# The second block's modulation as row sums on VectorE instead of matmuls on TensorE

## The chip, the cores and the metric

One core of a Trainium2 chip runs the whole program in one launch. The time is device time in microseconds (us) from the start to the end of one execution; the kernel before was timed in three runs, and a profile was taken of one further execution. The engines are TensorE (PE; its weight loads are listed as PEld), VectorE (DVE), ScalarE (ACT), GpSimd (POOL) and SyncE (SP), which here only issues DMA transfers, all of them on one queue.

## The reference

The input x is 256 tokens of 1024 features. A first block of two layers mixes them in four ways (stick-breaking attention, RWKV-7, block attention, HGRN-2), gates and sums the four branches, projects the sum out, and adds a feed-forward net with 2816 hidden columns. A second block follows, of one layer: it has latent attention and a two-directional mLSTM, and then 16 experts. All is float32.

The second block is modulated. A vector c of 1024 numbers (and c_ctx, for a context of 256 further tokens) gives six vectors of 1024 features each, the scales, shifts and gates of the second block's norms:

```
mod     = silu(c)     @ w_mod + b_mod      # w_mod: 1024 x 6144
mod_ctx = silu(c_ctx) @ w_mod + b_mod      # only scale and shift of the first norm are used
```

They depend on neither x nor the first block, so they can be computed at any time before they are used. w_mod has 25 MB, and each of its numbers is used once or twice.

## The kernel before

Activations lie with features on the partitions: x is [128, 8, 256], eight feature tiles of 256 tokens. A product takes a piece of a weight, 1024 rows by 256 columns, in two halves of 512 KB. `half_weights` (line 205) loads a half on SP's queue into one of four raw buffers, ScalarE copies it to a rounded high part (line 179 in `copy`), and VectorE, for every third half GpSimd, subtracts to get the low part (line 182 in `sub`). TensorE then does three matmuls for each pair of tiles, high by high, high by low and low by high (lines 227 to 229 in `mm3`). Raw, high and low parts have four buffers each, so at most two pieces are ready ahead of TensorE.

`layer` (line 878) runs twice. It makes the norm and the projections of the four mixers, weaves the mixers' chains with further projections (`weave`, line 867), then does the output projection (four pieces), the norm of the feed-forward net, its 22 gate and up pieces and the down projection (four column quarters of three pieces each). Layer 1 norms the context (`norm_mod` on cx) between the gate and up products and the down projection; this is where the modulation is used first. `second` (line 1180) and `moe` (line 1816) are the second block; the experts' weights, 192 pieces of 1 MB, come last.

The order of an engine's list is not quite the order of the code. The framework plans the lists at build time: it takes the instructions in the order of the code, but where an engine has nothing to do by its own estimate, it takes a later instruction whose inputs are there and whose buffers are free. On the chip each engine then runs its list strictly in order, and SP's queue of transfers is such a list.

The modulation is a generator (`modulation`, line 1130). silu(c) and silu(c_ctx) stand in two columns of zeros in `cp`, so that a matmul with 32 columns of `cp` as its weights and 256 columns of w_mod as its data (line 1155) puts a chunk's sums on two rows of one PSUM tile, in four groups of the array's columns. Each of 24 chunks takes four loads of 256 KB into buffers borrowed from other tiles (tags qk, am, t2, r2) and eight matmuls, which the profile lists as 16 records. Two rounds of 12 chunks each end in a copy, a turn by two small matmuls and an addition of b_mod. The code asks for seven chunks beside layer 0's mixers (`M0`), four ahead of layer 0's gate and up products (`M1`), the last chunk and the end of the first round at layer 1's norm, and the whole second round ahead of layer 1's gate and up products.

Of the kernel before, what the change touches and what calls it, by code (L numbers as in the profile page):

```python
# [9 lines left out]
F32 = mybir.dt.float32  # L10
# [23 lines left out]
def _const_table():  # L34
    """Masks, rotations and index tables that depend on the shapes alone."""
# [8 lines left out]
    # partial rotary, two heads of 64 on the partitions  # L44
# [16 lines left out]
    # chunks of 64 tokens on the partitions (two of them), 64 columns  # L61
# [17 lines left out]
    # partial sums of four column groups of the array: rows r, r + 32, r + 64, r + 96  # L79
# [9 lines left out]
def _const2_table():  # L89
# [3 lines left out]
    # axial rotary, two heads of 64 on the partitions  # L93
# [14 lines left out]
    # partial sums of four column groups of the array: rows r, r + 32, r + 64, r + 96  # L108
    # gate g of head h in direction d (row 8 d + 4 g + h of the sums) goes to partition 32 d + h
# [22 lines left out]
for _name, _n in [  # L132
    ("norm1_g", 16), ("norm2_g", 16), ("final_g", 8), ("mu", 16), ("w0", 4), ("a0", 4), ("k_k", 4),
    ("k_a", 4), ("r_k", 4), ("gn_w", 4), ("gn_b", 4), ("v0", 2), ("lb", 4), ("hgn", 4),
    ("c", 8), ("c_ctx", 8), ("b_mod", 48), ("norm1_2", 8), ("norm2_2", 8), ("final_2", 8),
    ("q_norm", 3), ("kv_norm", 2), ("conv_w", 40), ("conv_b", 8), ("ml_norm", 8), ("ml_skip", 8),
]:
    _PRM[_name] = (_NPRM, _n)
    _NPRM += _n


class Block:
# [53 lines left out]
    def split(self, hi, lo, src, scale=None, eng=None):  # L196
        """src = hi + lo exactly, in two parts that one pass of the array carries."""
# [7 lines left out]
    def half_weights(self, ap, parts=1):  # L205
        """A piece [128, n <= 1024] of a weight, split."""
# [12 lines left out]
    def weights(self, ap, n):  # L219
        """A piece [128, n] of a weight, split, in two halves."""  # L220
        h = n // 2
        parts = [self.half_weights(ap[:, i * h:(i + 1) * h]) for i in range(2)]
        return lambda c, w: parts[c // h](c % h, w)
# [7 lines left out]
    def proj_fm(self, ps, w, x, nk, nm, m0=0, width=None, k0=0, first=True, last=True):  # L231
        """ps[:, m*256:+256] (+)= columns m of w (feature-major), x = (hi, lo) [128, nk, 256]."""
# [7 lines left out]
    def proj_tok(self, ps, w, x, nk):  # L240
        """ps[:, j*256:+256] = tokens of tile j, 256 columns of w (token-major)."""
# [6 lines left out]
    def rstd(self, out, ps, n, eps):  # L248
        """out = (ps / n + eps) ** -0.5"""
# [3 lines left out]
    def rstd_small(self, out, ss, n, eps):  # L253
        """out = (ss / n + eps) ** -0.5, on VectorE"""
# [4 lines left out]
    def rsqrt(self, out, x):  # L259
        """out = x ** -0.5: a first guess from the exponent, then two steps of Newton's kind."""  # L260
# [11 lines left out]
    def square_sums(self, x, w=None, cols=1):  # L272
        """[128 tokens, j, c]: sums over the features of w(k)[:, c] * x ** 2, by column groups of the array."""
# [14 lines left out]
    def spread(self, r, out):  # L288
        """Factors by token [128, nj] on every partition: out [128, nj * 128] in PSUM."""
# [4 lines left out]
    def rms8(self, x):  # L294
        """(mean of x ** 2 over the 8 feature tiles + 1e-6) ** -0.5 on every partition."""
# [5 lines left out]
    def rms(self, squares, n, eps, nj=2):  # L301
        """(sum of the squares over the features / n + eps) ** -0.5 of nj * 128 tokens, on every partition."""
# [32 lines left out]
    def norm_split(self, x, nk, n, eps, gcol, hi, lo, bias=None, r=None):  # L335
        """hi + lo = x * rstd * g (+ bias), over the nk feature tiles of x."""
# [12 lines left out]
    def att_out(self, att, v, hp, hh, yhi, ylo):  # L349
        """o^T = v^T att^T of two heads; att [128 s, 2, 384]: (s0: t 0..255), (s1: t 128..255)."""  # L350
# [7 lines left out]
    def stick(self, got, y):  # L358
        """q is scaled by 1/8."""
# [29 lines left out]
    def tri(self, t):  # L389
        """Zero where s >= t in the diagonal blocks of t [128 s, 2, (t0, t1 of s0, t1 of s1)]."""  # L390
# [4 lines left out]
    def rotate(self, x, rot, cos, sin, n):  # L395
        """x [128, n, 256] in place."""
# [47 lines left out]
    def lower_bounds(self):  # L444
        """lb[:, 0:2] of layer 0, [:, 2:4] of layer 1; and 1 - lb."""
# [20 lines left out]
    def hgrn(self, l, q, f, got, room, y):  # L466
        """q, f, sg = silu(g) * 2 feature-major [128, 2, 256]; v token-major."""
# [18 lines left out]
        # scores by keys: [64 cc + s, head parity, 2 * head pair + tile, query of the same 64 tokens]; the first  # L486
        # half of a tile against its second half; the first tile against the second
# [44 lines left out]
        # sums of the products with the first 64 keys of a tile in one bank, with the others in the next  # L532
        o, v = self.mx(), got["v"]
        for hp in range(2):
            for j in range(2):
# [7 lines left out]
                # the first into each half of the partitions clears what the bank has seen before  # L543
# [21 lines left out]
    def rwkv(self, l, pz, y):  # L565
        """pz: four pieces [128, 2, 256] of the projected columns."""
# [53 lines left out]
        # unit key, key, bonus  # L620
# [25 lines left out]
        # decays within chunks of 64  # L646
# [33 lines left out]
        # instance (h, c): h = 2 hp + hh, c = 2 j + cc; its tokens lie on partitions 64 cc..  # L680
# [36 lines left out]
        def prod(lh, rh):  # L717
            """lh^T rh of each instance: both on the tokens' partitions; bank = chunk parity."""
# [7 lines left out]
        for m in (2, 4, 8, 16, 32):  # L726
            # what the chain below needs only later fills its gaps
# [34 lines left out]
        # U0 = X (A_ak V), W = X a  # L762
# [23 lines left out]
        # the state's matrices: on the features' partitions, column (cc, hp, j)  # L786
# [15 lines left out]
        # diag(P_C): eye * pc, column order (cc, hp, j)  # L802
# [64 lines left out]
    def weave(self, streams):  # L867
        """Emits the streams side by side; each comes with about its number of steps, and its start among the others."""
# [9 lines left out]
    def layer(self, l, x):  # L878
# [4 lines left out]
        if l == 0:  # L883
            # x * g for the first two products; their results take the tokens' factors
# [3 lines left out]
            for i in range(2):  # L888
                # the first weights' halves follow the halves of x that they meet
# [7 lines left out]
            # the array is cold: its sums take squares that are added before  # L897
# [11 lines left out]
        if l:  # L909
            self.mod_tags = ("qk",)  # L910
            for _ in islice(self.mods, 2):
                pass
# [90 lines left out]
        def branch(n, first):  # L1003
            """mg (+)= 2 sigmoid(gate) * (y @ w_branch) of mixer n."""
# [21 lines left out]
        if l == 0:  # L1026
            mods = self.mods = self.modulation()
            self.mod_tags = ("qk",)
            streams.append((islice(mods, M0), MO, MS))
# [5 lines left out]
        for k in range(8):  # L1035
            self.split(mh[:, k], ml[:, k], mg_[:, k], scale=0.5)
        for c in range(4):
            ps = self.acc()
# [4 lines left out]
        # the products take x * g; their results the tokens' factors  # L1043
# [4 lines left out]
        self.mod_tags = ("am", "t2", "r2", "r2")  # L1048
        for _ in islice(self.mods, M1 if l == 0 else 26):
            pass  # L1050
# [10 lines left out]
        for c in range(4):  # L1061
            ps = self.mx()
            for g, (k0, n) in enumerate(((0, 8), (8, 8), (16, 6))):
                w = self.weights(a["w_down"][l, c][:, 256 * k0:256 * (k0 + n)], 256 * n)
# [6 lines left out]

    def silu_mul(self, ps, r, hi, lo):
        """hi + lo = silu(r * ps[:, :256]) * (r * ps[:, 256:])"""
# [46 lines left out]
    def slabv(self, *dims, dt=F32, pool=None):  # L1120
        """A view of 8 KB a partition, of the slabs that stay or of the second block's."""
# [8 lines left out]
    def modulation(self):  # L1130
        """mod[:, i, 0] of c and [:, i, 1] of c_ctx: column tile i of silu(c) @ w_mod + b_mod."""
        T, S, V = self.T, self.S, self.V
        # c and c_ctx stand in columns 22 and 23 of zeros: chunk q of a round takes 32 columns so that
        # its sums go to the rows 2 q and 2 q + 1, beside those of the round's other chunks
# [935 lines left out]
```

## Time and profile before

| | |
|---|---|
| median of three runs | 1905.74 us (1903.93 to 1913.77) |
| span of the profiled execution, first to last instruction | 1908.3 us |
| TensorE's weight loads, busy | 1345.3 us (71%) |
| VectorE, busy | 916.8 us (48%) |
| ScalarE, busy | 720.2 us (38%) |
| GpSimd, busy | 456.5 us (24%) |
| mean granted TensorE clock, of full speed | 0.929 |
| bytes moved by the DMA engines | 416.91 MB, mean 218 GB/s |

The page gives nothing of the profiled execution outside its span, so the span stands for its own time; it lies between the timed runs. Busy time is the union of an engine's instructions. Matmuls overlap in the records (one of 0.28 us starts every 0.12 us), so sums of single durations are larger than busy times. Layer 0 lasts from the start to about 550 us, layer 1 from there to about 1090 us, the second block's attention and mLSTM to about 1450 us, and the experts to the end.

### The profile page before, as it was taken

What the parts mean: (1) busy time and instruction counts of PE and PEld (TensorE: products, weight loads), DVE (VectorE), ACT (ScalarE), POOL (GpSimd) and SP (SyncE); (2) the same over time, 40 slices, a digit from 0 to 9 for tenths busy, and PEclk for the clock granted to TensorE, in tenths of its full rate; (3) what the DMA queues carried; (4) which work ended last, traced back from release to release, by engine and by line L of the source; (5) the groups of instructions that cost most, each with busy time, mean ns of one, the idle gap of its engine ahead of it and who ended that gap; (6) DMA issues with size and microseconds to landing.
All of it is one profiled execution on the core that took longest, in us unless ns stands there. A gap on an engine that the chain in (4) does not pass through costs nothing. (4 is left out here: it accounts for less than half of the span.)

```text
span 1908.3 us, 34087 instructions
## 1 busy us (share of the span) xinstructions
PE 1695.0 (89%) x14380; PEld 1345.3 (71%) x14380; DVE 916.8 (48%) x1395; ACT 720.2 (38%) x1136; POOL 456.5 (24%) x285
## 2 busy tenths in 40 slices
PE   7799899999999899999999999989997976667666
PEld 7668799999989788997998998867896410101113
DVE  8755645577557756553776448453574100000001
ACT  5535544444446454543444343554443200000001
POOL 4352143244323622431442221111231000000000
PEclk9899999999999899999999999989999977776788
DMA  6552546455645226566554643322457999999997
GB/s 228 167 171 92 167 154 200 146 176 177 180 153 162 84 86 194 165 219 228 169 177 137 184 136 126 100 72 74 164 209 298 427 426 427 427 427 428 426 427 329
DMA packets 96379, 416.91 MB, mean 218 GB/s; under 512 B 10689, under 2 KB 12385, under 8 KB 71521
## 3 DMA queue, kind: packets, MB, share of 16 engines
q1 hardware_dynamic: 96224, 414.72, 60.3%
q8 instruction: 113, 1.85, 0.4%
q14 instruction: 42, 0.34, 0.1%
HBM read 413.63 MB, written 1.05 MB: 217 GB/s over the span
## 5 line engine op out<-in xcount | busy, mean ns | idle before, releaser
L227 PE MATMUL acc<-s,wh 128*128 128x256 f32 (+1 forms) x2236 | 652.3, 292 | 12.6 <-ACT wh L179 8.6
L228 PE MATMUL acc<-s,wh 128*128 128x256 f32 (+1 forms) x2236 | 647.7, 290 | 4.8 <-DVE s L191 4.0
L229 PE MATMUL acc<-s,wl 128*128 128x256 f32 (+1 forms) x2236 | 647.7, 290 | 0.0
L179 ACT ACTIVATE wh<-wr 128x1024 fp32r<-128x1024 f32 (+2 forms) x349 | 359.4, 1036 | 343.1 <-PE acc L228 203.0
L227 PEld LDWEIGHTS acc<-s,wh 128*128 128x128 f32 x2236 | 436.2, 195 | 29.1 <-issue 15.7
L228 PEld LDWEIGHTS acc<-s,wh 128*128 128x128 f32 x2236 | 436.4, 195 | 15.6 <-issue 8.0
L182 POOL TENSOR_TENSOR wl<-wr,wh 128x1024 fp32r<-128x1024 f32 (+1 forms) x115 | 282.7, 2458 | 658.5 <-ACT wh L179 589.9
L229 PEld LDWEIGHTS acc<-s,wl 128*128 128x128 f32 x2236 | 436.2, 195 | 3.8 <-issue 1.8
L182 DVE TENSOR_TENSOR wl<-wr,wh 128x1024 fp32r<-128x1024 f32 (+2 forms) x234 | 304.4, 1302 | 240.1 <-ACT wh L179 238.9
L1831 PE MATMUL mx<-s,s 128*32 128x512 f32 x608 | 103.3, 766 | 39.4 <-DMA s<-in_w_moe_dram 39.4
L1831 PE MATMUL mx<-mw,s 128*32 128x512 f32 x416 | 76.2, 809 | 36.3 <-DMA mw<-in_w_moe_dram 36.3
L1831 PEld LDWEIGHTS mx<-s,s 128*32 128x32 f32 x608 | 14.5, 120 | 112.3 <-DMA s<-in_w_moe_dram 96.3
L1831 PEld LDWEIGHTS mx<-mw,s 128*32 128x32 f32 x416 | 9.7, 122 | 92.1 <-DMA mw<-in_w_moe_dram 88.1
L188 POOL TENSOR_TENSOR t<-t,rr 128x256 f32<-128x256 f32 x44 | 42.8, 972 | 127.5 <-DVE t L188 124.8
L191 DVE SCALAR_TENSOR_TENSOR x<-acc,mod,x 128x256 f32<-128x256 f32 x28 | 12.2, 480 | 104.2 <-PE acc L1839 100.8
L188 DVE TENSOR_TENSOR m<-m,mx 128x1024 f32<-128x1024 f32 x4 | 4.9, 1222 | 114.5 <-PE mx L1831 114.5
L227 PE MATMUL mx<-r,wh 128*128 128x256 f32 x208 | 59.0, 284 | 0.0
L228 PE MATMUL mx<-r,wh 128*128 128x256 f32 x208 | 58.8, 282 | 0.0
L229 PE MATMUL mx<-r,wl 128*128 128x256 f32 x208 | 58.6, 282 | 0.0
L191 DVE SCALAR_TENSOR_TENSOR m<-m,mx 128x1024 f32<-128x1024 f32 x4 | 4.9, 1220 | 107.5 <-ACT m L1862 107.5
L1831 PE MATMUL mx<-s,ht 128*32 128x512 f32 x224 | 39.2, 794 | 17.9 <-DMA s<-in_w_moe_dram 17.8
L191 DVE SCALAR_TENSOR_TENSOR t<-t,t 128x256 f32<-128x256 f32 (+1 forms) x46 | 46.9, 1019 | 12.4 <-ACT t L1076 8.2
(516 smaller groups left out, 2534.6 us busy)
## 6 DMA issues: line engine op xcount, KB each, us to landing
s<-in_w_moe_dram SPq DMA_DIRECT2D x110, 1024.0 KB, 19.6
mw<-in_w_moe_dram SPq DMA_DIRECT2D x81, 1024.0 KB, 19.6
wr<-in_w_in_dram SPq DMA_DIRECT2D x158, 512.0 KB, 4.1
wr<-in_w_gu_dram SPq DMA_DIRECT2D x88, 512.0 KB, 4.3
wr<-in_w_down_dram SPq DMA_DIRECT2D x32, 512.0 KB, 4.2
wr<-in_w_out_dram SPq DMA_DIRECT2D x24, 512.0 KB, 3.9
qk<-in_w_mod_dram SPq DMA_DIRECT2D x32, 256.0 KB, 3.1
wr<-in_w_branch_dram SPq DMA_DIRECT2D x16, 512.0 KB, 4.1
```

Source lines behind the costliest of these rows:

```text
L179: self.S.activation(out, in_, AF.Copy)
L182: (eng or self.V).tensor_tensor(out, a, b, op=ALU.subtract)
L188: (eng or self.V).tensor_tensor(out, a, b, op=ALU.mult)
L191: self.V.scalar_tensor_tensor(out, a, s, b, op0=op0, op1=op1)
L227: T.matmul(out, wh, xh, start=start, stop=False)
L228: T.matmul(out, wh, xl, start=False, stop=False)
L229: T.matmul(out, wl, xh, start=False, stop=stop)
L1831: T.matmul(ps[32 * e:32 * e + 32], lhs(k, e), w[:, e * 512:(e + 1) * 512], start=k == 0, stop=k == 7, tile_position=(0, 32 * e))
```

## The change

The matmuls of the modulation go. w_mod is laid out transposed on the host, [48, 128, 1024]: column tile i, its 128 columns on the partitions, the 1024 rows along the free dimension. c and c_ctx come as one array of two rows, and one transfer spreads it over all partitions (`cb`). Then one VectorE instruction multiplies a tile of w_mod by silu(c), both in SBUF, writes the products to a tile that nobody reads (`junk`) and their sum along the row to a column of `mod`. The first 16 column tiles get two such sums, c_ctx and c, the other 32 one. The tiles of w_mod have two buffers of their own; a load is asked for one step ahead.

The steps are asked for ahead of each piece of the output and the down projections: one each in layer 0 (16 steps) and two each in layer 1 (32 steps). To make room, the space set aside for GpSimd's transfers is cut to 256 bytes. c and c_ctx leave the table of parameters. Comments that the diff takes out are left out here, and so are the constants that go.

```diff
@@ layer
-        if l:
-            self.mod_tags = ("qk",)
-            for _ in islice(self.mods, 2):
-                pass
...
-        if l == 0:
-            mods = self.mods = self.modulation()
-            self.mod_tags = ("qk",)
-            streams.append((islice(mods, M0), MO, MS))
         self.weave(streams)
...
+        if l == 0:
+            self.mods = self.modulation()
         for c in range(4):
+            self.some(1 + l)
             ps = self.acc()
             self.proj_fm(ps, self.weights(a["w_out"][l, c], 2048), (mh, ml), 8, 2)
...
-        self.mod_tags = ("am", "t2", "r2", "r2")
-        for _ in islice(self.mods, M1 if l == 0 else 26):
-            pass
...
             for g, (k0, n) in enumerate(((0, 8), (8, 8), (16, 6))):
+                self.some(1 + l)
                 w = self.weights(a["w_down"][l, c][:, 256 * k0:256 * (k0 + n)], 256 * n)
...
+    def some(self, n):
+        for _ in islice(self.mods, n):
+            pass
...
@@ modulation (the new body; the old one goes)
+        S, V = self.S, self.V
+        cb = self.act.tile([128, 2, 1024], F32, name="cb")
+        junk = self.act.tile([128, 1024], F32, name="junk")
+        self.nc.sync.dma_start(cb, self.a["cc"][None, :, :].to_broadcast([128, 2, 1024]))
+        for j in range(2):
+            S.activation(junk, cb[:, j], AF.Tanh, scale=0.5)
+            self.stt(cb[:, j], junk, 1.0, cb[:, j], ALU.add, ALU.mult)
         self.mod = self.const.tile([128, 48, 2], F32, name="mod")
         o, _ = _PRM["b_mod"]
+        def load(i):
+            w = self.act.tile([128, 1024], F32, tag="wmod", name="wmod", bufs=2)
+            self.nc.sync.dma_start(w, self.a["w_mod"][i])
+            return w
+
+        w = load(0)
+        for i in range(48):
+            w, cur = load(i + 1) if i < 47 else None, w
+            for j in (1, 0) if i < 16 else (0,):
+                V.scalar_tensor_tensor(junk, cur, 0.5, cb[:, j], op0=ALU.mult, op1=ALU.mult, accum_out=self.mod[:, i, j:j + 1])
+            if i in (15, 47):
+                n = 2 if i == 15 else 1
+                r = slice(0, 16) if i == 15 else slice(16, 48)
+                self.add(self.mod[:, r, 0:n], self.mod[:, r, 0:n],
+                         self.prm[:, o + r.start:o + r.stop][:, :, None].to_broadcast([128, r.stop - r.start, n]))
             yield
...
@@ arrays, kernel
-    g["w_mod"] = _cols(i["w_mod_2"][0], 256)
+    g["w_mod"] = np.ascontiguousarray(i["w_mod_2"][0].T).reshape(48, 128, 1024)
+    g["cc"] = np.stack([i["c_2"][0], i["c_ctx_2"]])
...
-    nc = bacc.Bacc("TRN2", target_bir_lowering=False, num_devices=1)
+    nc = bacc.Bacc("TRN2", target_bir_lowering=False, num_devices=1, dynamic_dma_scratch_size=256)
```

## Rows read from the trace of the kernel before

**Rows 1.** The page: TensorE's busy time in all, and in 40 slices (tenths).

```profile
PE 1695.0 (89%) x14380; PEld 1345.3 (71%) x14380; DVE 916.8 (48%) x1395; ACT 720.2 (38%) x1136; POOL 456.5 (24%) x285
...
PE   7799899999999899999999999989997976667666
```

**Rows 2.** Windows, line 1155 alone: stretch, length, busy us (records) by engine, clock, DMA.

```profile
60.00:140.00 80.00, 19.30 (x112) 4.23 (x112) 0.91 0.53 168
345.00:360.00 15.00, 4.87 (x64) 2.60 (x64) 1.00 0.50 159
874.00:899.00 25.00, 16.32 (x192) 6.94 (x192) 1.00 0.71 244
0.00:1908.30 1908.30, 42.57 (x384) 14.61 (x384) 0.93 0.61 218
```

**Rows 3.** Waits of TensorE's matmuls: waiter, awaited, us in all, times, longest.

```profile
PE wm L1155 <- DMA qk<-in_w_mod_dram: 9.2, 2, 8.1
...
PE wm L1155 <- DMA r<-in_w_mod_dram: 1.2, 1, 1.2
```

**Rows 4.** Timeline at anchors: start, us, engine, line, operation, idle before it.

```profile
68.04 0.48 PE L591 MATMUL sm<-t,lora 128*128 128x256 f32 x1
...
76.85 0.64 PE L1155 MATMUL wm<-qk,cp 128*32 128x256 f32 x2 [8.11 <-DMA qk<-in_w_mod_dram]
...
351.82 0.69 DVE L185 TENSOR_TENSOR x<-x,acc 128x512 f32<-128x512 f32 x1 [0.41 <-PE acc L229]
...
610.92 0.48 PE L591 MATMUL sm<-t,lora 128*128 128x256 f32 x1
...
874.15 0.69 DVE L185 TENSOR_TENSOR x<-x,acc 128x512 f32<-128x512 f32 x1 [0.41 <-PE acc L229]
```

**Rows 5.** Windows, all lines: PE, PEld, DVE, ACT, POOL busy, clock, DMA.

```profile
40.00:140.00 100.00, 86.89 (x927) 66.18 (x929) 68.40 (x80) 42.68 (x68) 43.55 (x24) 0.93 0.57 181
140.00:240.00 100.00, 92.78 (x1333) 81.36 (x1332) 59.76 (x87) 54.02 (x74) 21.71 (x19) 0.98 0.41 132
240.00:345.00 105.00, 102.75 (x839) 101.38 (x840) 54.27 (x64) 50.48 (x73) 40.01 (x19) 0.98 0.54 174
345.00:475.00 130.00, 128.79 (x1097) 125.33 (x1096) 88.84 (x118) 59.19 (x89) 50.99 (x32) 1.00 0.52 166
600.00:680.00 80.00, 68.64 (x849) 61.42 (x848) 62.69 (x72) 40.58 (x66) 43.03 (x24) 0.91 0.32 106
60.00:140.00 80.00, 66.89 (x735) 46.38 (x737) 49.60 (x56) 28.63 (x49) 36.02 (x21) 0.91 0.53 168
1062.26:1077.83 15.57, 15.57 (x135) 15.57 (x134) 6.56 (x5) 5.94 (x6) 4.24 (x2) 1.00 0.62 189
874.00:899.00 25.00, 23.62 (x252) 13.09 (x251) 4.20 (x14) 5.23 (x11) 1.45 (x1) 1.00 0.71 244
```

**Rows 6.** Instructions by line: count, ns min/median/max, first and last start, shapes.

```profile
L191 DVE SCALAR_TENSOR_TENSOR t<-t,t x46: 411/421/2473, 366.8 to 1033.2; 128x256 f32<-128x256 f32 x44, 128x256 fp32r<-128x256 f32 x2
...
L191 DVE SCALAR_TENSOR_TENSOR s<-th,y x8: 679/684/2070, 1159.7 to 1206.7; 128x512 f32<-128x512 f32 x8
...
L485 DVE TENSOR_TENSOR_SCAN t<-cst,t x4: 658/678/2890, 53.8 to 602.9; 128x256 f32<-128x256 f32 x4
...
L426 ACT ACTIVATION_READ_ACCUMULATOR s<-s,st x16: 184/187/188, 230.3 to 778.6; 128x1 f32 x16
```

**Rows 7.** Timeline: VectorE's low parts, without and beside GpSimd's.

```profile
1064.73 1.22 DVE L182 TENSOR_TENSOR wl<-wr,wh 128x1024 fp32r<-128x1024 f32 x1
...
1069.09 2.46 DVE L182 TENSOR_TENSOR wl<-wr,wh 128x1024 fp32r<-128x1024 f32 x1 [0.33 <-ACT wh L179]
```

**Rows 8.** Timeline: instructions that ran ahead of their place in the code.

```profile
0.78 0.47 POOL L1136 MEMSET cp<- 128x448 f32 x1 [0.29 <-POOLq L2060]
...
727.00 1.31 SPq L1151 DMA_DIRECT2D am<-in_w_mod_dram  x2
...
776.30 0.15 DVE L191 SCALAR_TENSOR_TENSOR c<-mod,prm 128x8 f32<-128x8 f32 x1
```

More of the change, by code (lines that the diff above doesn't have):

```diff
@@ L134 @@
     ("k_a", 4), ("r_k", 4), ("gn_w", 4), ("gn_b", 4), ("v0", 2), ("lb", 4), ("hgn", 4),
-    ("c", 8), ("c_ctx", 8), ("b_mod", 48), ("norm1_2", 8), ("norm2_2", 8), ("final_2", 8),
+    ("b_mod", 48), ("norm1_2", 8), ("norm2_2", 8), ("final_2", 8),
     ("q_norm", 3), ("kv_norm", 2), ("conv_w", 40), ("conv_b", 8), ("ml_norm", 8), ("ml_skip", 8),
@@ L1130, in modulation @@
     def modulation(self):
-        T, S, V = self.T, self.S, self.V
-        cp = self.act.tile([128, 8, 56], F32, name="cp")
-        self.G.memset(cp, 0.0)
-        for j, nm in enumerate(("c", "c_ctx")):
-            o, _ = _PRM[nm]
-            c = self.prm[:, o:o + 8]
-            t = self.tmp.tile([128, 12], F32, tag="st", name="c8", bufs=4)[:, 0:8]
-            S.activation(t, c, AF.Tanh, scale=0.5)
-            self.stt(t, t, 1.0, c, ALU.add, ALU.mult)
-            self.ts(cp[:, :, 22 + j], t, 0.5, None, ALU.mult, ALU.bypass)
+        S, V = self.S, self.V
@@ L1144, in modulation @@
+        cb = self.act.tile([128, 2, 1024], F32, name="cb")
[4 more added lines that the diff above has]
+            self.stt(cb[:, j], junk, 1.0, cb[:, j], ALU.add, ALU.mult)
         self.mod = self.const.tile([128, 48, 2], F32, name="mod")
         o, _ = _PRM["b_mod"]
-        for r in range(2):
-            ps = self.wm()
-            for q in range(12):
-                for n in range(4):
-                    raw = self.t2(self.mod_tags[n % len(self.mod_tags)])
-                    self.nc.sync.dma_start(raw, self.a["w_mod"][12 * r + q][:, n * 512:(n + 1) * 512].rearrange("p (a b) -> p a b", a=2))
-                    for m in range(2):
-                        k = 2 * n + m
-                        c = 32 * (k % 4)
-                        T.matmul(ps[c:c + 32, 0:256], cp[:, k, 22 - 2 * q:54 - 2 * q], raw[:, m], start=q == 0 and k < 4,
-                                 stop=q == 11 and k >= 4, tile_position=(0, c))
-                yield
-            t = self.t1()
-            self.copy(t, ps[:, 0:256])
-            pm = self.wm()
-            for m in range(2):
-                T.matmul(pm[:, 24 * m:24 * m + 24], t[:, m * 128:(m + 1) * 128], self.C("sel24"))
-            V.tensor_tensor(self.mod[:, 24 * r:24 * r + 24].rearrange("p (i m) w -> p m i w", m=2),
-                            pm[:, 0:48].rearrange("p (m i w) -> p m i w", m=2, w=2),
-                            self.prm[:, o + 24 * r:o + 24 * r + 24].rearrange("p (i m) -> p m i", m=2)[:, :, :, None].to_broadcast([128, 2, 12, 2]),
-                            op=ALU.add)
@@ L1948 @@
 SEQ_ = "bbbpppppbbbABb0123456"
-M0 = 7
-M1 = 4
-MO = 48.2
 WEAVE = [tuple(zip(w[:3], w[3:])) for w in ((38, 22.4, 15, 0, 0.0, 0), (31.3, 17.6, 14.9, 0, 0, 0.0))]
@@ L1963 @@
 BV = 1
-MS = 0.13
 NS = 3
@@ L1995, in arrays @@
         "lb": i["hgrn_lb_logits"], "hgn": i["hgrn_gn_g"],
-        "c": i["c_2"], "c_ctx": i["c_ctx_2"], "b_mod": i["b_mod_2"], "norm1_2": i["norm1_2"],
+        "b_mod": i["b_mod_2"], "norm1_2": i["norm1_2"],
         "norm2_2": i["norm2_2"], "final_2": i["final_norm_2"], "q_norm": i["q_norm_2"],
```

## Prediction

> **What bounds the kernel now.** I read the page's totals and slices first, then the modulation's own matmuls by stretch, their waits, the timeline at two anchors, and VectorE's idle time where the new work could go. TensorE is busy 89% of the span, and the slices (47.7 us each) show it at 8 tenths and more from 95 to some 1430 us [rows 1]; behind that the stream of expert weights sets the pace. What ends the first block earlier moves everything behind it by as much, so the question is what the modulation costs TensorE inside the first block. The reader is to see three things: where its 42.57 us of busy time lie [rows 2], that TensorE once stood still for 8.11 us because of one of its loads [rows 3, 4], and that the same layer code runs faster the second time, when no modulation is woven into it [rows 4].
>
> **What the change removes.** All 384 matmul records of line 1155 go, and the 96 loads of 256 KB that feed them, two copies and two small additions. Three places matter.
>
> A, the first layer's mixers. Between 60 and 140 us the modulation keeps TensorE busy for 19.30 us [rows 2] and waits once for 8.11 us, during which VectorE and ScalarE run dry too. From both sides: nothing, if TensorE would stand idle there without it, to 19.30 + 8.11 = 27.4 us. To choose, I compare the layers, which run the same code: from the second LoRA product to the addition of the output projection's last piece, layer 0 takes 351.82 - 68.04 = 283.8 us and layer 1, which has no modulation in that stretch, 874.15 - 610.92 = 263.2 us [rows 4]. The difference is 20.6 us, and I take it. Two other windows speak for the same size: in 80 us of the same chains TensorE is busy 68.64 us in layer 1 and 66.89 us in layer 0, of which 19.30 are modulation [rows 5], so layer 1 does some 21 us more of the real work in equal time.
>
> B, ahead of layer 0's gate and up products: 4.87 us in 345 to 360 us [rows 2], right behind the output projection's end at 351.82 [rows 4], with the gate and up products next on the list, so all of it counts. From the other side, the norm's sums stand in the same stretch and could show up in its place; at worst nothing is gained.
>
> C, layer 1's norm: the rest, 42.57 - 19.30 - 4.87 - 16.32 = 2.1 us [rows 2]. It fills TensorE's wait for the norm, so I count 0, with 2.1 as the bound.
>
> D, ahead of layer 1's gate and up products: from 874 to 899 us the modulation is busy 16.32 us [rows 2], and TensorE idles another 25.00 - 23.62 = 1.4 us [rows 5]. The weights of the next product have been split by then, and VectorE has only 4.20 us of work in the stretch. Together 17.7 us; the bounds are 16.3 and 17.7, less the few microseconds that the norm's own sums may take instead. I take 17.7.
>
> Sum of the gains: 20.6 + 4.9 + 0 + 17.7 = 43.2 us.
>
> **What it adds.** 64 row sums over 128x1024 on VectorE (two for each of the first 16 column tiles, one for each of the other 32), 48 loads of 512 KB, one load that spreads c and c_ctx over all partitions, two tanh and two products for their silu. The bytes stay (48 x 512 KB against 96 x 256 KB). The two tanh and the spreading load have nothing behind them that is due soon; I count them 0.
>
> One sum: the trace has no VectorE instruction with an accumulated output. A subtraction of two inputs over 128x1024 takes 1.22 us [rows 7]; reading an accumulator out takes 0.187 us on ScalarE [rows 6], the nearest row there is. Lower bound 1.22; upper bound from the scan, which takes 678 ns for 256 columns where the same operation without a running value takes 421 [rows 6]: 1.22 + 4 x 0.257 + 0.19 = 2.44 us. I take 1.22 + 0.19 = 1.41 us, as the form of the instruction is that of the 421 ns row. 64 x 1.41 + 2 x 1.22 = 93 us of VectorE.
>
> The Trainium skill has a rule against this: "Vector Engine (DVE) Microarchitecture Reference", section "Points that are easy to get wrong", says that a scalar-tensor-tensor instruction with two SBUF sources that are not bf16 runs at half throughput, because nothing is left for reading back the accumulator. By it a sum takes about 2.4 us. Without an accumulated output the rows disagree: two SBUF sources take 421 ns for 256 columns and 684 for 512 [rows 6], 1.03 ns for each further column, with no halving in it; with an accumulated output, no row here tells. What it would do is a rival below.
>
> Where the sums will stand is the choice that matters most. The code asks for them piece by piece in both layers' output and down projections. But the planner that orders the engines' lists moves work forward as soon as inputs and buffers are free: the zeros of cp, asked for where layer 0's mixers begin, are written at 0.78 us; weights that are multiplied from 874 us on are loaded at 727; the scale of the context's norm, asked for ahead of layer 1's down projection, is computed at 776 [rows 8]. The sums' tiles have buffers of their own from the start. So I expect most sums in VectorE's idle time of layer 0's mixers: between 40 and 345 us it idles 31.6 + 40.2 + 50.7 = 122.5 us, and 41.2 us more until 475 [rows 5]. 93 us fit.
>
> That is not free. A sum cannot be broken off, so an instruction of the mixers' chains that becomes ready meanwhile waits half a sum, 0.7 us, on average. Of the idle time 71.8 of 122.5 us lie ahead of 240 us, where the chains still hold TensorE up (92.78 us busy of 100, against 102.75 of 105 behind it) [rows 5]; so 38 of the 64 sums count. 38 x 0.7 = 27 us of delay; two chains run side by side, and I put half of it, 13 us, on the path. Bounds: 0 (TensorE's other work covers it) and 64 x 0.7 = 45 us.
>
> VectorE also waits for loads in order. TensorE waited 9.2 + 1.2 = 10.4 us for 96 loads of the modulation [rows 3], so 48 loads cost 5 us; bounds 0 and two waits like the longest, 16 us. Behind a waiting sum stand the chains, the low parts of the split weights and the additions to x. A load into one of the two buffers stands on SP's only queue until the sum two tiles before is done, and the mixers' weight loads stand behind it; that cover is four half pieces, and its loss is the slower rival.
>
> GpSimd takes every third low part, and VectorE does nothing with two SBUF inputs meanwhile: a subtraction of 1.22 us took 2.46 beside one of GpSimd's [rows 7]. A sum will be held up so at times; I add 1 us.
>
> If the sums do stay in the projections, a column quarter of the down projection has 15.57 us, of which VectorE uses 6.56 (1.2 of them held up) and GpSimd 4.24 [rows 5]; six sums add 8.5, so 18.1 us are to be done one at a time in 15.57. Eight quarters lose 8 x 2.5 = 20 us at most, and the two output projections much the same per piece, half of it covered by split weights that lie ready: the total is near that of the chosen case.
>
> Costs: 13 + 5 + 1 = 19 us. Net 43.2 - 19 = 24 us. The profiled span is 1908.3 us, 2.6 above the median of 1905.7, with runs from 1903.9 to 1913.8; 1884.3 of its kind is 1882 as a median.
>
> **Rivals.** (1) The sums disappear in idle time: costs near 4, gain 40, 1866 us. For it: VectorE's idle 122.5 us; against it: the chains use VectorE most where they hold TensorE up. (2) Layer 0's modulation filled TensorE's idle time anyway: A gives nothing, 22.6 - 19 = 4 us gained, 1902 us. For it: chains bound that stretch; against it: layer 1. (3) The sums take 2.44 us each, the upper bound: 64 x 2.44 + 2.4 = 159 us, more than the idle 122.5; the rest spills into layer 0's gate and up products, and half lengths of 1.2 us cost 38 x 1.2 / 2 = 23, with 10 for the spill (by the 41.2 us of idle time there against 36 that come) and the waits together 33: 43.2 - 33 = 10 us gained, 1896 us. The Trainium skill's rule above would lead here. (4) Slower: SP's queue is held by the modulation's loads. Each of 46 loads waits for a sum, 1.41 us; if the queue has no slack, weights come late by that: 46 x 1.5 = 69 us against 43.2, so 26 slower, 1932 us. It decides from 43.2 / 46 = 0.94 us per load. For it: the wait of 8.11 us [rows 4] was for a load of just this kind; against it: all 96 loads of before cost 10.4 us [rows 3].
>
> **How the numbers follow.** Forecast 46%, (1) 13%, (2) 14%, (3) 12%, (4) 15%. Half a percent (9.5 us, about what the runs can tell from no change) puts the borders at 1896 and 1915. Faster: nearly all of the forecast and (1), half of (3), a little of (2): 0.65. Same: most of (2), the other half of (3), the forecast's upper end: 0.20. Slower: (4) and a little of (2): 0.15. The range goes from the gains at their bounds with small costs, 43.2 + 6.8 - 4 = 46 gained, 1860, to past (2) and (3), 1912; (4) is left out. The likeliest case alone: 1868 to 1896.
>
> **What would show it.** A: from the LoRA products to the last addition, layer 0 near 265 us plus the costs; no wait of 8 us in 60 to 100 us. D: gate and up products beginning at once behind the output projection. The sum: its mean, near 1.2 us and a read-out of about 0.2. Place: the sums' first and last start; before 60 and near 350 us by my account. Costs: TensorE waiting for VectorE or the split weights in layer 0's mixers. The prediction is wrong if A gives nothing, if loads of weights come late on SP's queue, or if a sum takes 2 us and more.

## The result, and the profile after

The changed kernel is slower, by 0.7%: 1921.8 us median (1916.1 to 1924.0) against 1906.2 for the kernel before on the same chip, ratio 1.0074 with a 95% interval from 1.0049 to 1.0100. The forecast was 1882, and 1912 the upper end of its range.

The page after (TensorE's and VectorE's rows, then slices of 48.0 us), against [rows 1]:

```profile
PE 1673.8 (87%) x13988; PEld 1342.8 (70%) x13988; DVE 1023.1 (53%) x1521; ACT 720.2 (37%) x1134; POOL 470.4 (24%) x284
...
PE   6768899999999889999999999989997976666666
...
DVE  8889787767646866645676548453574100000001
```

TensorE's first five slices fell from 7 7 9 9 8 tenths to 6 7 6 8 8 (windows of 40 to 345 us follow); behind them the rows are alike. Windows over all lines after, against the first three of [rows 5]:

```profile
40.00:140.00 100.00, 75.25 (x860) 69.75 (x858) 88.52 (x105) 45.94 (x71) 48.40 (x24) 0.85 0.47 152
140.00:240.00 100.00, 81.48 (x1181) 71.14 (x1181) 86.02 (x123) 42.56 (x55) 27.33 (x18) 0.95 0.56 170
240.00:345.00 105.00, 98.28 (x734) 91.80 (x733) 85.76 (x109) 45.45 (x65) 39.31 (x17) 0.93 0.71 233
```

VectorE (third busy time) now works 82 to 89% of these stretches where it worked 52 to 68%, and TensorE lost 27.4 us of work there (282.4 to 255.0), more than the modulation's own 19.3 [rows 2]. The sums by line after, durations in ns as minimum, median, maximum:

```profile
L1151 DVE SCALAR_TENSOR_TENSOR junk<-wmod,cb x64: 1183/1225/3412, 56.6 to 336.6; 128x1024 f32<-128x1024 f32 x64
L1151 DVE DVE_READ_ACCUMULATOR junk<-wmod,cb x64: 72/80/84, 59.7 to 337.8; 128x1 f32 x64
```

All 64 stand in layer 0's mixers, as forecast. The anchors of [rows 4] in the timeline after:

```profile
75.68 0.70 PE L591 MATMUL sm<-t,lora 128*128 128x256 f32 x2
...
380.94 0.69 DVE L185 TENSOR_TENSOR x<-x,acc 128x512 f32<-128x512 f32 x1 [0.41 <-PE acc L229]
...
640.21 0.70 PE L591 MATMUL sm<-t,lora 128*128 128x256 f32 x2
...
899.56 0.69 DVE L185 TENSOR_TENSOR x<-x,acc 128x512 f32<-128x512 f32 x1 [0.41 <-PE acc L229]
```

Layer 0's stretch takes 380.94 - 75.68 = 305.3 us against 283.8, and starts 7.6 us later; its end is 29.1 us late. Layer 1's takes 259.4 against 263.2. What waits between 40 and 385 us after (the second fence has SP's queue):

```profile
DVE junk L1151 <- DMA wmod<-in_w_mod_dram: 20.0, 14, 3.7
PE mx L723 <- POOL am L742: 12.2, 2, 9.0
...
PE sm L626 <- ACT r L624: 4.6, 1, 4.6
PE mx L498 <- ACT t L474: 4.3, 1, 4.3
...
PE mx L691 <- DVE am L693: 3.9, 1, 3.9
```

```profile
SPq L214 <- DVE wl L182: 110.0, 43, 6.5
...
SPq L1143 <- DVE junk L1151: 69.0, 34, 7.0
```

TensorE's wait for a modulation load [rows 3] is gone; it waits for steps of the mixers' chains instead, 51.7 us over all its lines against 22.2 before in 40 to 385 us. The longest of these waits is for GpSimd, which works through five steps of a chain beside sums. The five, of which the first and the last are shown, take 10.5 us there; before (second fence) they took 6.7, and in e1, the run without modulation below, 8.6. TensorE's wait for the last of them is 9.01 us after and 3.9 in e1:

```profile
116.40 2.18 POOL L712 TENSOR_TENSOR am<-am,cst 128x512 f32<-128x512 f32 x1 [1.23 <-DVE am L693]
...
119.06 2.28 DVE L1151 SCALAR_TENSOR_TENSOR junk<-wmod,cb 128x1024 f32<-128x1024 f32 x1
...
124.62 2.25 POOL L742 TENSOR_TENSOR am<-am,cst 128x512 f32<-128x512 f32 x1
...
126.92 0.58 PE L723 MATMUL mx<-am 64*64 64x64 f32 x6 [9.01 <-POOL am L742]
```

```profile
113.03 1.27 POOL L712 TENSOR_TENSOR am<-am,cst 128x512 f32<-128x512 f32 x1 [1.23 <-DVE am L693]
...
118.43 1.26 POOL L742 TENSOR_TENSOR am<-am,cst 128x512 f32<-128x512 f32 x1
```

So the sums hold GpSimd up as well. From 40 us to the addition of the output projection's last piece, its 62 instructions take 125.69 us after and 107.99 in e1 (fifth busy time; then the clock):

```profile
40.00:380.94 340.94, 288.95 (x3041) 266.29 (x3043) 285.65 (x365) 152.71 (x221) 125.69 (x62) 0.91 0.58 186
```

```profile
40.00:339.31 299.31, 274.05 (x3059) 255.28 (x3062) 188.23 (x237) 152.03 (x221) 107.99 (x62) 0.96 0.40 125
```

Where the time came from, by stage: the start of the load of one and the same weight in each run, in us against the kernel before, where these loads start at about 330, 487, 593, 771, 907 and 1131 us; the last column is the span's end.

| run | end of layer 0's mixers | end of its gate and up | start of layer 1 | end of its mixers | in its gate and up | second block | end |
|---|---|---|---|---|---|---|---|
| after | +29.2 | +29.9 | +29.3 | +26.9 | +11.9 | +12.5 | +13.3 |
| e1, no modulation | -11.0 | -13.0 | -13.0 | -15.3 | -30.3 | -31.2 | -26.4 |
| e2, loads alone | +11.9 | +10.0 | +9.6 | +6.8 | -8.2 | -10.5 | -8.3 |
| e3, sums alone | +20.9 | +20.3 | +19.8 | +17.4 | +2.4 | +1.5 | +4.8 |
| e4, in gate and up | -9.5 | +15.5 | +14.3 | +12.0 | -4.1 | +17.5 | +20.8 |
| e5, as asked | -11.8 | -5.4 | +11.1 | +11.3 | +3.1 | +32.0 | +34.7 |
| e7, loads unread | -9.0 | -9.6 | -9.4 | -9.5 | -23.0 | -22.5 | -22.7 |

### The profile page after: what moved, and what is told of

It is laid out like the page before. It is cut to its first block, busy times and chain, and to the rows that moved or that the text cites. A ratio compares the mean times of both kernels' runs of the same rounds, so it can differ in the third digit from the quotient of the medians.

```text
span 1921.6 us, 33382 instructions
## 1 busy us (share of the span) xinstructions
PE 1673.8 (87%) x13988; PEld 1342.8 (70%) x13988; DVE 1023.1 (53%) x1521; ACT 720.2 (37%) x1134; POOL 470.4 (24%) x284
## 5 line engine op out<-in xcount | busy, mean ns | idle before, releaser
L227 PE MATMUL acc<-s,wh 128*128 128x256 f32 (+1 forms) x2236 | 655.7, 294 | 16.8 <-ACT wh L179 8.6
L227 PEld LDWEIGHTS acc<-s,wh 128*128 128x128 f32 x2236 | 438.5, 196 | 32.6 <-issue 14.5
L1821 PE MATMUL mx<-s,s 128*32 128x512 f32 x608 | 107.5, 794 | 39.8 <-DMA s<-in_w_moe_dram 39.8
L1151 DVE SCALAR_TENSOR_TENSOR junk<-wmod,cb 128x1024 f32<-128x1024 f32 x64 | 97.7, 1527 | 20.7 <-DMA wmod<-in_w_mod_dram 20.0
L188 POOL TENSOR_TENSOR t<-t,rr 128x256 f32<-128x256 f32 x44 | 42.8, 973 | 134.2 <-DVE t L188 134.2
L188 DVE TENSOR_TENSOR m<-m,mx 128x1024 f32<-128x1024 f32 x4 | 4.9, 1222 | 115.9 <-PE mx L1821 115.9
L227 PE MATMUL mx<-r,wh 128*128 128x256 f32 x208 | 59.6, 286 | 0.0
```

The source lines that it names most:

```text
L188: (eng or self.V).tensor_tensor(out, a, b, op=ALU.mult)
L227: T.matmul(out, wh, xh, start=start, stop=False)
L1151: V.scalar_tensor_tensor(junk, cur, 0.5, cb[:, j], op0=ALU.mult, op1=ALU.mult, accum_out=self.mod[:, i, j:j + 1])
L1821: T.matmul(ps[32 * e:32 * e + 32], lhs(k, e), w[:, e * 512:(e + 1) * 512], start=k == 0, stop=k == 7, tile_position=(0, 32 * e))
```

## The experiments

Ratios are to the kernel before, with 95% intervals. "Sums' cost" below is a run's median less that of a kernel without modulation whose low parts are split in the same way: e1 or e10, and e16 for e15 and e18. For e17 it is e1, which differs from it in one more line.

**e1 to e4: what goes and what comes.**

```
e1  modulation(): only  mod = b_mod
e2  scalar_tensor_tensor(junk[:, 0:8], cur[:, 0:8], 0.5, cb[:, j, 0:8], ...)
e3  w = [load(0), load(1)];  cur = w[i % 2]
e4  hold(x[:, 7, 0:1]) ahead of gate and up; some(1 or 2) beside its pieces; factor 0.5 -> self.gate
    hold(v): gate = v * 0 + 0.5
```

> Left out: all row sums and their loads; the modulation is its bias alone. Times against before 1906 and after 1922. Theory V (the row sums, standing in layer 0's mixers, take more of VectorE than the chains there leave, so that TensorE waits): taking them all away gives what the prediction counted as gains, 43 us, 1863. Rival R (layer 0's modulation on TensorE only filled idle time, so removing it gives nothing there): D alone, some 14 to 20 us, 1886 to 1892. Rival Q (the loads hold SP's queue) says the same as V here: 1863.

Measured: 1883.0 us, ratio 0.9875 (0.9858 to 0.9892). 23 us come back, not 43. The anchors of e1's timeline:

```profile
70.71 0.70 PE L591 MATMUL sm<-t,lora 128*128 128x256 f32 x2
...
339.31 0.69 DVE L185 TENSOR_TENSOR x<-x,acc 128x512 f32<-128x512 f32 x1 [0.41 <-PE acc L229]
...
597.90 0.70 PE L591 MATMUL sm<-t,lora 128*128 128x256 f32 x2
...
857.39 0.69 DVE L185 TENSOR_TENSOR x<-x,acc 128x512 f32<-128x512 f32 x1 [0.41 <-PE acc L229]
```

Without any modulation layer 0 still takes 268.6 us where layer 1 takes 259.5: 9 of the 20.6 us between the layers [rows 4] were never the modulation's. The end of layer 0's mixers comes 12.5 us earlier. Neither V's 1863 nor R's 1886 to 1892 fits; it lies nearer to R.

> Left out: each row sum reads only 8 of its 1024 columns; the 48 loads of 512 KB and their order stay. Theory V: VectorE's work is nearly gone, so within 10 us of the kernel without modulation, near 1870. Rival Q: the loads themselves cost the time, near 1915.

Measured: 1898.3 us, ratio 0.9962 (0.9946 to 0.9978); 15 us above e1, between V and Q. One row of its waits in 40 to 380 us says why; no wait for a weight's load is among its rows:

```profile
DVE junk L1151 <- DMA wmod<-in_w_mod_dram: 42.5, 23, 4.6
```

> Left out: only two of the 48 tiles are loaded, all 64 row sums of full length read these two. Theory V: nearly all of the cost stays, less the 20 us in which VectorE waited for loads, of which I put half on the path: near 1912. Rival Q: near 1870, since nothing is left on SP's queue.

Measured: 1915.1 us, ratio 1.0049 (1.0028 to 1.0071); 32 us above e1, as V said. The two prices, 15 and 32, don't add up to the full 39: a sum that waits for its load and a sum that works may hold the list in the same moments, which was not shown.

> Everything is computed; each row sum takes its factor 0.5 from a column that depends on x as it stands behind the layer's output projection, so that none can run in the mixers: 16 tiles (32 sums) beside layer 0's gate and up products, 32 tiles (32 sums) beside layer 1's. Theory V: no chain waits for VectorE there and 4 half pieces of split weights lie ready, so the sums cost less than 12 us of the 43 gained: 1865 to 1876. Rival Q: the loads stand on the same queue between the weights' loads and hold them as before, 1910 or more. Rival R: 1886 to 1895.

Measured: 1928.1 us, ratio 1.0117 (1.0099 to 1.0135). This was a miss for V: the mixers ran nearly as in e1, but layer 0's gate and up products lost 25 us over 32 sums. TensorE's longest waits there are for VectorE emptying the result bank of a piece (`PE acc L227 <- DVE t L188`, 16.4 us in nine waits), not for weights.

**e5 to e8: place, GpSimd, bandwidth, length.**

```
e5  some() where the code has it; hold(mg_[:, 7, 0:1]) ahead of the output projection, hold(ff[21] low) ahead of down
e6  NS = 3 -> NS = 1000        (low parts: every third on GpSimd -> none)
e7  the scalar_tensor_tensor and the two additions of b_mod go; mod = b_mod
e8  for h, m in ((0:512, mod), (512:1024, rest)): scalar_tensor_tensor(junk[:, h], cur[:, h], ..., accum_out=m[...])
```

> Everything is computed; each row sum takes its factor 0.5 from a column that depends on the last mixer output (output projections) or on the last gate and up product (down projections), so that the sums stand where the code asks for them: 8 sums beside each layer's output projection, 24 beside each down projection. Theory V (the cost is VectorE's time and its waits in layer 0's mixers): those mixers run as without modulation; a down projection's column quarter takes 18.1 us where it took 15.6, eight of them 20 us, the output projections a few: 1903 to 1908. Rival W (a sum costs some 0.6 us wherever it stands, by 39 us over 64 sums, as the ones beside the gate and up products did): 1922.

Measured: 1942.1 us, ratio 1.0181 (1.0155 to 1.0208), slower than either. Layer 0's down projection lost 16.5 us over 24 sums and layer 1's 29 over 24 with a load each (table). TensorE's longest waits in layer 0's down projection are for VectorE's low parts, queued behind the sums:

```profile
PE mx L229 <- DVE wl L182: 10.4, 4, 3.7
```

> The changed kernel, but the low parts of all split weights are subtracted on VectorE, none on GpSimd. Theory P (what is short is the time in which neither VectorE nor GpSimd works, since a sum and a subtraction on GpSimd do not run at once): a low part that took 2.46 us on GpSimd takes 1.22 on VectorE, and sums run their 1.22 undisturbed: 19 us of sums' delay and some 20 x 1.2 us of the mixers' low parts come back, half of it on the path: 1900 to 1912. Rival V1 (VectorE's own list is short, GpSimd takes work off it): a third of the low parts more on VectorE, 20 x 1.22 us in layer 0's mixers alone: 1935 and more.

Measured: 1859.9 us, ratio 0.9754 (0.9734 to 0.9774): 62 us off the changed kernel, far more than P said. The sums run less disturbed (longest 2317 ns, not 3412), but much of the gain lies behind them; e9 and e10 sort this out.

> Left out: the row sums; the 48 loads stay, with nothing that reads them, so that VectorE never waits for them and SP never for VectorE. Theory V: the 15 us that the loads cost beside 8-column sums were VectorE's waits in its list; 1883 to 1887. Rival B (the transfers take bandwidth from the weights' loads): near 1898.

Measured: 1883.4 us, ratio 0.9870 (0.9843 to 0.9897), the time of e1. The transfers cost nothing by themselves, so bandwidth is out.

> Everything is computed; each row sum is done as two of 512 columns, added at the end. Rival N (the prediction's own term: an instruction of the chains waits half a sum, because a sum cannot be broken off): half lengths bring back half of that term, 6 to 10 us: 1912 to 1916. Theory V (VectorE's time and waits): nothing comes back and 64 more instructions cost their fixed time, 0.1 us each: 1922 to 1930.

Measured: 1931.8 us, ratio 1.0128 (1.0103 to 1.0153), 10 us slower than whole sums. Rival N's 6 to 10 us do not come back, but the run does not decide on rival N, the prediction's own reading of its 13 us. In 37 of the 64 sums the second half follows the first with nothing between them, so no instruction could slip in. And the halves keep VectorE busy longer, 127.6 us against 97.7: the median is 686 ns, the mean 1031, as GpSimd holds halves up too.

**e9 to e11: the same with GpSimd out of the low parts.** Each is one edit, NS = 1000, in the kernel before, e1 and e4.

> The kernel before, with all low parts on VectorE and none on GpSimd; nothing else is changed. Of the 62 us that this brought to the changed kernel, some 26 lay behind layer 0's mixers, where hardly a sum stands, and should come here too. Theory P (it is with GpSimd's subtractions that the sums collide): in layer 0's mixers little comes back without sums, so 1870 to 1880, and the change itself gains 10 us or more once GpSimd stands aside. Rival F (GpSimd's subtractions cost the mixers as much without the sums): 1843 to 1850, and the change stays a loss of 10 us.

Measured: 1858.6 us, ratio 0.9730 (0.9712 to 0.9747).

> Left out: all row sums and their loads; and all low parts are on VectorE. What the modulation's sums still cost in the changed kernel with all low parts on VectorE (1860) is the difference to this. Theory P: the sums cost 10 to 15 us then, against 39 beside GpSimd: 1845 to 1850. Rival F: they cost 30 or more: 1830 or less.

Measured: 1829.9 us, ratio 0.9580 (0.9566 to 0.9595).

> Everything is computed; the sums are held to the gate and up products of both layers, as in the run that took 1928, and all low parts are on VectorE. Theory P: the gate and up products then leave VectorE 39 us of 155, against 25 us that both engines left together before; most sums fit: 1850 to 1862. Rival F or V1: VectorE's own time is short there, 1890 or more.

Measured: 1868.9 us, ratio 0.9785 (0.9769 to 0.9802), a little outside P's range.

GpSimd's low parts cost the kernel before some 50 us and e1 53, with no sum near them. So most of e6 was not the sums' doing; P falls for the greater part. With GpSimd aside TensorE's modulation costs 29 us and the sums 30: no difference (the intervals of e6 and e9 overlap). The sums alone still need explaining, in the mixers (e6) and beside the gate and up products (e11, 39 us).

**e12 to e14: bunched or not.**

```
e12  e4 with one sum per gate and up piece, held by the piece before it, 2 or 3 per down quarter; NS = 1000
e13  the same, NS = 3
e14  the changed kernel, for i in range(16); mod[:, 16:48] = b_mod
```

> Everything is computed; all low parts on VectorE; each row sum is held by its factor so that one at most stands beside a gate and up piece (22 in each layer), and two or three beside a column quarter of the down projections (10 in each layer). Against 1830 without modulation and 1860 and 1869 with the sums bunched. Theory H (the sums cost because they stand in bunches: their list takes all of VectorE's time for 100 us and more on end): 1832 to 1842. Rival W (each sum costs about half its length wherever it stands): 1860 to 1870.

Measured: 1861.5 us, ratio 0.9779 (0.9751 to 0.9806).

> The same spread of the sums, with GpSimd's share of the low parts as in both kernels. Theory H: 1885 to 1897, faster than before (1906) by the 23 us of removal less a few. Rival W: 1915 to 1925. If GpSimd's subtractions alone are the reason, this one is slow (1915 and more) and the run with all low parts on VectorE fast.

Measured: 1926.7 us, ratio 1.0114 (1.0088 to 1.0139).

> Left out: the row sums and loads of tiles 16 to 47, so 32 sums and 16 loads remain, where the planner puts them. Theory H (it is the share of VectorE's time that counts; half the sums leave it idle time enough): 1884 to 1893, against 1883 without any. Rival W: half of the 39 us, 1902.

Measured: 1904.5 us, ratio 1.0004 (0.9991 to 1.0017); 21.5 us for 32 sums.

Theory H falls in all three: 0.5 to 0.7 us per sum, spread or not, half as many or not. But e12's timeline shows what a gate and up piece consists of. VectorE alone, one period, from sum to sum:

```profile
391.39 1.28 DVE L1154 SCALAR_TENSOR_TENSOR junk<-wmod,gate,cb 128x1024 f32<-128x1024 f32 x1
...
392.60 0.42 DVE L188 TENSOR_TENSOR t<-acc,rr 128x256 f32<-128x256 f32 x1
392.93 1.22 DVE L182 TENSOR_TENSOR wl<-wr,wh 128x1024 fp32r<-128x1024 f32 x1
394.07 0.42 DVE L191 SCALAR_TENSOR_TENSOR t<-t,t 128x256 f32<-128x256 f32 x1
394.52 0.42 DVE L188 TENSOR_TENSOR t<-t,acc 128x256 f32<-128x256 f32 x1
394.86 1.22 DVE L182 TENSOR_TENSOR wl<-wr,wh 128x1024 fp32r<-128x1024 f32 x1
397.16 0.42 DVE L191 SCALAR_TENSOR_TENSOR r<-t,r 128x256 fp32r<-128x256 f32 x1 [1.08 <-ACT r L202]
...
397.81 1.28 DVE L1154 SCALAR_TENSOR_TENSOR junk<-wmod,gate,cb 128x1024 f32<-128x1024 f32 x1
```

The period is 6.42 us, as in 18 of layer 0's 21, and VectorE's list, with a wait of 1.08 us in it, fills it without a gap. In e10, without sums, the product that empties a piece's bank comes every 5.76 us, and it is VectorE that waits, for TensorE:

```profile
378.08 0.42 DVE L188 TENSOR_TENSOR t<-acc,rr 128x256 f32<-128x256 f32 x1 [0.34 <-PE acc L229]
...
383.84 0.42 DVE L188 TENSOR_TENSOR t<-acc,rr 128x256 f32<-128x256 f32 x1 [0.35 <-PE acc L229]
```

The wait of 1.08 us in e12 is for a chain through ScalarE and GpSimd (`POOL t L188`, 1.59 us). VectorE is not busy all the time, but its list, in order, has no room.

**e15 to e18: a shorter list.**

```
e15  e12;  silu_mul: mul(u, u, r, eng=self.G) -> mul(u, u, r);  held by ff[j - 2], not ff[j - 1]
e16  e10 with the same line in silu_mul
e17  e15 with NS = 3
e18  e6 with the same line in silu_mul (sums not held)
```

> Everything is computed; the spread sums with all low parts on VectorE (1861), and in the gate and up pieces the product with the norm's factor goes from GpSimd to VectorE, and a sum hangs on the piece before the last one. There a piece took 6.42 us, with VectorE busy 5.6 of them and waiting 1.1 for ScalarE behind GpSimd's product of 1.6; without sums a piece takes TensorE 5.7. Theory L (VectorE's in-order list, its waits in it, is what a piece lasts): the waits go, a piece fits again into about 5.7 us, and the 16 us that the sums cost in both layers' gate and up products come back: 1843 to 1850. Rival W: unchanged, 1858 to 1863.

Measured: 1835.2 us, ratio 0.9632 (0.9600 to 0.9665). Theory L holds, but its range is missed by 8 us, as more came back than it said: the sums cost 5 us in all. One period of e15:

```profile
394.85 1.28 DVE L1154 SCALAR_TENSOR_TENSOR junk<-wmod,gate,cb 128x1024 f32<-128x1024 f32 x1
...
396.06 0.42 DVE L188 TENSOR_TENSOR t<-acc,rr 128x256 f32<-128x256 f32 x1
396.40 1.22 DVE L182 TENSOR_TENSOR wl<-wr,wh 128x1024 fp32r<-128x1024 f32 x1
...
400.61 1.28 DVE L1154 SCALAR_TENSOR_TENSOR junk<-wmod,gate,cb 128x1024 f32<-128x1024 f32 x1
```

It takes 5.76 us again. The same 100 us, 340 to 440, in e12 and in e15 (stretch, length, PE, PEld, DVE, ACT, POOL busy, clock, DMA):

```profile
340.00:440.00 100.00, 95.28 (x776) 93.34 (x775) 83.67 (x145) 44.09 (x63) 22.16 (x15) 1.00 0.66 206
```

```profile
340.00:440.00 100.00, 100.00 (x835) 100.00 (x835) 97.57 (x174) 51.77 (x70) 0.00 (x0) 1.00 0.70 224
```

VectorE is busier in e15, 97.6 of 100 us, and TensorE waits for nothing: it was the order and the waits in the list that cost, not the busy time. Two edits went together here, the product's engine and the piece that a sum hangs on; which did more was not tried.

> Left out: all row sums and their loads; all low parts and the product with the norm's factor on VectorE. The control for the run before it: TensorE never waited in this loop without sums, so unchanged by theory L: 1828 to 1832. Anything faster would mean that GpSimd's product cost time by itself.

Measured: 1830.5 us, ratio 0.9606 (0.9569 to 0.9643), as e10. The shorter list gains nothing by itself.

> Everything is computed; as the run that took 1835 (spread sums, the norm's factor multiplied on VectorE), but every third low part is on GpSimd again, as in both kernels. If the shorter list in the gate and up pieces was all that the sums needed, 5 us above the 1883 without modulation: 1885 to 1893. If the collisions of the sums with GpSimd's subtractions cost as well: 1900 to 1915.

Measured: 1913.8 us, ratio 1.0044 (1.0029 to 1.0059), 31 us above e1. With GpSimd's low parts back, a sum of e17 lasts up to 3.3 us beside one of them, and the next piece is held up with it:

```profile
396.04 2.40 POOL L182 TENSOR_TENSOR wl<-wr,wh 128x1024 fp32r<-128x1024 f32 x1 [6.96 <-DVE r L191]
...
396.20 3.32 DVE L1154 SCALAR_TENSOR_TENSOR junk<-wmod,gate,cb 128x1024 f32<-128x1024 f32 x1
```

> Everything is computed; the changed kernel with all low parts and the norm's factor on VectorE, its sums not held, so in layer 0's mixers where the planner puts them. Theory V (place matters: there VectorE is in the chains): the 28 us of those mixers stay, 1856 to 1862. Rival (the shorter list was the whole gain, place does not matter): 1835 to 1840.

Measured: 1860.7 us, ratio 0.9760 (0.9739 to 0.9781), as e6: in layer 0's mixers the 30 us stay. So place, list and GpSimd all count, and of the combinations tried only all three together bring the sums' cost near nothing (in us):

| sums stand | low parts on GpSimd too | all low parts on VectorE |
|---|---|---|
| layer 0's mixers (planner) | 39 | 30 |
| gate and up, bunched | 45 | 39 |
| gate, up and down, spread | 44 | 32 |
| the same, shorter list | 31 | 5 |

e15 beats both kernels, and also e9, the kernel before with its low parts on VectorE (0.9632 against 0.9730): there the change gives 23 us, about the 24 that were forecast for it. That is luck: it is the sum of 29 us gained and 5 lost, not of 43 and 19.

## Why the prediction was wrong

The sign was wrong by two steps, of nearly equal weight; sizes of the first block's stages are at the trace's anchors.

**Step A mis-sized.** "The difference is 20.6 us, and I take it": e1 gives 12.5 at the end of the mixers, where the stretch is 15.2 us shorter and begins 2.7 us later. The comparison of the layers took all that differs for the modulation; 9 us of it stay in e1, and what they are was not tried. The wait of 8.11 us [rows 4] and 19.30 us of busy time [rows 2] stood in that stretch, and taking both away gave 12.5 to 15.2 of their 27.4. The chains pace it: without the modulation, TensorE's waits for other steps in 40 to 385 us rise from 22.2 - 9.2 = 13.0 us to 27.1. A filler there costs less than its busy time.

**B, C, D.** B was forecast at 4.9 and gave 0.6, near the lower bound that I named. C was 0 and gave 0.6: e1's matmuls start 12.4 us earlier ahead of layer 1's norm and 13.0 behind it. D was 17.7 and gave 13.5 (16.8 earlier ahead of it, 30.3 behind it); behind layer 1's output projection TensorE now waits for the norm, 2.19 us at once in e1. The 3.7 us between 13.0 and 16.8 came in layer 1's mixers and output projection, where no matmul of the modulation ran. Three of them lie from 755 to 761 us, where the granted clock before is 0.50 (1.2 GHz) and a matmul starts every 0.21 us; for the same matmuls in e1 the clock is 1.00 (2.4 GHz), and one starts every 0.12 us. In both runs they stand behind a wait of 1.23 us. At layer 1's gate and up products e1 is 30 us ahead, against 43.2. Five of these are gone again at the end of the program (table), and the medians differ by 23; why was not tried.

**The sums' cost: 19 forecast, 39 measured, 41.6 at the end of the mixers.** The step that failed is "38 x 0.7 = 27 us of delay; two chains run side by side, and I put half of it, 13 us, on the path". e3 puts this term at 32, nearer to the upper bound of 64 x 0.7 = 45 us that I gave beside it; neither the 38 nor the half held. All sums count: e14's 32, which stand ahead of 193 us, cost 21.5 us, and the other 32, from 203 us on in the changed kernel, add 17. "93 us fit" into 122.5 us of idle time was the error under it. Almost half of that idle time before (40 to 345 us) is one kind of wait, of a low part for its high part, and the rest are shorter waits, mostly for steps of the chains:

```profile
DVE wl L182 <- ACT wh L179: 57.2, 27, 9.2
```

Such time has a fixed place in the list, and what is put in ahead of an instruction delays it when it outlasts the wait. That this is why a sum in the mixers costs 0.5 us is argued; a period was written down for the gate and up pieces alone, and the share of GpSimd's lengthened steps was not separated.

**The sum's length was right.** 1225 ns in the median, and 80 ns of read-out that lies beside the next instruction; I had 1.41 us. Rival (3) is out: the Trainium skill, "Vector Engine (DVE) Microarchitecture Reference", section "Points that are easy to get wrong", has such an instruction at half throughput; 1024 columns in 1225 ns, the time of the subtraction in [rows 7], show none of it here.

**The load waits were too small.** "48 loads cost 5 us": VectorE waited 20.0 us for them, and e2 and e7 put the price of waiting in order, without the sums' own time, at 15.

**GpSimd's "1 us" too.** Sums took 97.7 us in all, not 64 x 1.23 = 78; held up, up to 3.4 us. The Trainium skill, "SBUF — State Buffer", section "Who interferes with whom", says that a VectorE instruction with two SBUF inputs contends with a GpSimd one that reads SBUF, and that the port pair they share is an exclusive lock. The traces agree (3.32 us in e17, 2.46 in [rows 7]). I knew the row and put 1 us on it. The other direction had no term: the sums add 18 us to GpSimd's work in layer 0's mixers and stand beside TensorE's longest wait, 9.01 us. And what GpSimd's share costs the kernel without any sums, some 50 us, I did not ask.

**Rival (4) was right in sign, not in cause.** SP's queue did stand 69.0 us for sums, the very number of its sum but in 34 waits and not 46, which is luck, and ScalarE waited 13.7 us for weights' loads in 40 to 385 us, against 2.1 before. But e3 has no such queue and still costs 32 of the 39 us, so some 7 are left for it, and in e2 the loads that come late are the modulation's own. Place was right (56.6 to 336.6 us), and leaving the sums in the projections, "near that of the chosen case", costs 59 (e5).

## What to carry to other kernels

Do not count idle time of an engine with an in-order list as room until its period is written down: add up one period of the list with the waits in it, and compare it with the engine that paces (here 6.42 against 5.76 us). Price a removed filler at the pacing chain, by a run without it, not by its busy time or by a sister stage. And where VectorE and GpSimd both read SBUF, try the work on VectorE alone first: GpSimd's help cost some 50 us here before any sum was added.

## What the hardware showed beyond expectation

An accumulated output costs VectorE next to nothing: 1225 ns for 1024 columns, and a read-out of 80 ns that starts some 0.07 us ahead of the sum's recorded end, together with the next instruction (both at 392.60 in e12). 48 loads of 512 KB into layer 0's mixers cost no time when nothing waits for them (1883.4 against 1883.0). Where TensorE lost work, its granted clock was lower as well, 0.85 after against 0.93 before in 40 to 140 us [rows 5], as a mean over its two levels of 1.2 and 2.4 GHz. It was 0.68 in 117.9 to 126.9 us, where TensorE waited 9.01 us for GpSimd. To the end of the mixers it is 0.91 over 341 us after and 0.96 over 299 us in e1. If all of that time were TensorE's at full work, 0.09 x 341 - 0.04 x 299 = 19 us of the 41.6 would go with the clock; this estimate from the two rows is an upper bound, as TensorE stood idle in part of it, and the share was not separated further.
